# Statistics, casts and attention loads of a two-block layer spread over turns: one core, float32 in two parts

## The chip, the cores and the metric

One NeuronCore of a Trainium2 chip runs the whole program. The metric is the device time of one execution in microseconds (us), median of three runs. Engines are named as the profile names them: PE is TensorE (PEld its weight loads), DVE is VectorE, ACT is ScalarE, POOL is GpSimd, SP is SyncE, which here only starts transfers.

## What is computed

Two blocks, each on 1024 tokens of width 1024, in float32. The first block, shortened:

```python
h = rms_norm(x, norm_g)
u = h @ w_in                       # v_c b_c c_c z_c q k v z_a gate_logits
y_a = (b_c * causal_conv(c_c * v_c) * silu(z_c)) @ w_conv_out
q, k = rms_norm(q, q_norm_g), rms_norm(k, k_norm_g)    # 16 and 4 heads of 64
o = sliding_window_attention(q, k, v, sinks) * silu(z_a)   # window 128, blocks of 128
y_b = o @ w_attn_out
merged = sigmoid(g_a) * y_a + sigmoid(g_b) * y_b
x = x + merged @ w_out
```

The second block adds to x a mixer (pooling and gated linear attention), a cross attention to 256 memory tokens, and a feed-forward layer of width 2816 with a causal convolution, each behind its own norm; the last step is a norm.

## The kernel before

Features lie on the 128 partitions, tokens along the rows, in two halves of 512. An activation is a grid of 8 feature tiles by 2 halves. Every matrix product is taken in three matmuls: each operand is split into a high part (a cast on ACT) and a low part (a subtraction on DVE), and high x high, high x low and low x high are summed in PSUM (`mm3`).

Large projections of the first block and the feed-forward layer go through `wino`: two output tiles of both halves by seven products of four feature tiles each (12 matmuls a product, 84 in all) instead of eight. The products want four sums or differences of activation tiles, T1 to T4, in high and low parts. `sums` makes them: T1 = T3's first tile less T1's, and so on, four tiles each. A product whose T is not ready spins through turns (`while b not in X: tick()`).

The order of the work is written out by hand. `tick()` is a **turn**: it finishes a weight page's low part, advances the making of a pair's weights by a step, and advances each generator in the list `side` by one `yield`. Dense products call it in their middle and after their end, `wino` after each product. Each engine works in the order of the program; a wait stops all that stands behind it on that engine.

The order in the first block is: k and v from x itself (the norm's factor is applied later), while `second_half` and `x_thread` make hT, the normalised x, half by half; z of the attention (four tiles dense, then pairs with `wino`); four pairs of q; four pairs of the gates; sixteen of the convolution; four more of the gates; then `co`, the convolution's output product, 8 weight pages per half, during which the generator `attention` runs in turns; then `ao`, the attention's output product.

`hT_sums` waits until hT is complete, loads all 16 tiles of hT again from DRAM copies (`hraw`, stored by `x_thread`) and runs `sums` on them in place. In the feed-forward layer `ffn_norm` runs `sums` on its own tiles.

`q_out` evacuates one q tile: ACT squares it (`qsq`), ACT writes the high part, DVE the low part. Its generator `stats` stores both parts to DRAM, gives the squares to PE (L882, head sums by a block of ones), and DVE and POOL make the norm's factor from that. It is advanced in the turn that follows the evacuation at once.

`att_in(p, h)` loads what one half of the heads p needs for one half of the tokens h: keys, four q tiles in two parts, values (for p = 0), four z tiles: 14 or 16 transfers, issued on POOL's queue. For h = 0 both calls stand ahead of the attention, for h = 1 inside it, at units 9 and 17. A `Unit` is a block of 128 queries and four heads; in turn i unit i makes scores, unit i - 1 the exponentials and the normalisation (POOL, L1103), unit i - 2 the transposes, unit i - 3 the values. In the first block of queries `scores` fills the score tile with a memset on POOL (L1066), and DVE then copies the valid scores into it (L1078).

Tiles come from rotating pools: `hp` 64 tiles of 512 columns, `tp` 8, `wpool` 2 per kind of weight page, and a region that is closed and opened again between stages (`hq`, `pg`). A tile is used again when its last reader is done. Weight pages (512 KB) are loaded on SP, two ahead.

Of the kernel before, what the change touches and what calls it, by code (L numbers as in the profile page):

```python
# [11 lines left out]
ALU = mybir.AluOpType  # L12
# [5 lines left out]
HT = 512  # L18
# [98 lines left out]
def _body(es, tc, nc, wp, vec, xT, memT, gk2, pw, cst, out, dbg):  # L117
# [9 lines left out]
    V, S, G, T = nc.vector, nc.scalar, nc.gpsimd, nc.tensor  # L127
# [29 lines left out]
    def dram(s, shape=(P, HT)):  # L157
        n = nm(s)
        return dpool.tile(list(shape), F32, name=n, tag=n)
# [8 lines left out]
    def f(ap):  # L168
        return ap.bitcast(F32)
# [6 lines left out]
    side = []  # L176
# [269 lines left out]
    def sums(t, X, hts):  # L446


        at = {"T1": (0, 0), "T2": (4, 1), "T3": (0, 1), "T4": (4, 0)}
        his, los = {}, {}  # L450

        def u(name, k):
            return t[at[name][0] + k, at[name][1]]

        def hi(name, k):
            his[name, k] = hts[name](name, F32R)
            S.copy(his[name, k], u(name, k))

        def lo(name, k):
            los[name, k] = hts[name](name, F32R)  # L460
            V.tensor_tensor(los[name, k], u(name, k), f(his[name, k]), ALU.subtract)  # L461
            if k == 3:
                X[name] = [(his[name, i], los[name, i]) for i in range(4)]

        for k in range(4):
            V.tensor_tensor(u("T1", k), u("T3", k), u("T1", k), ALU.subtract)
            V.tensor_tensor(u("T3", k), u("T3", k), u("T2", k), ALU.subtract)
            hi("T1", k)
            yield
        for k in range(4):  # L470
            V.tensor_tensor(u("T2", k), u("T2", k), u("T1", k), ALU.subtract)
            lo("T1", k)
            hi("T2", k)
            yield
        for k in range(4):
            lo("T2", k)
            V.tensor_tensor(u("T4", k), u("T4", k), u("T2", k), ALU.subtract)
            hi("T3", k)
            yield
        for k in range(4):  # L480
            lo("T3", k)
            hi("T4", k)
            if k:
                lo("T4", k - 1)
            yield
        lo("T4", 3)

    def reload(items, s, first=4, per=2, lag=3):

# [150 lines left out]
    xs = grid(KT)  # L640
# [27 lines left out]


    hR, hT = grid(KT), grid(KT)  # L670
    hraw = {}
    nrms = [Norm(), Norm()]
    rx = [None, None]

# [12 lines left out]
    def x_thread(h):  # L687

        rx[h] = rstd_cols([nrms[h].acc], 4, D, "o")
        for _ in range(3):  # L690
            yield
        R = bcast_cols(rx[h], 4, "s")
        yield
        sp = Splits(pool=True)
        for kt in range(KT):
            t = tp("xn")
            V.scalar_tensor_tensor(t, xs[kt][h], col("norm_g", kt), R, ALU.mult, ALU.mult)
            hT[kt][h] = [None, None]
            sp.add(t, hT[kt][h], "xn")
            hraw[kt, h] = dram("hraw")  # L700
            nc.sync.dma_start(hraw[kt, h], t)
            if kt % 2:
                yield
        sp.flush()

    kp = [(pg("kh", F32R), pg("kl", F32R)) for _ in range(2)]
# [125 lines left out]

    XB = {}

    def hT_sums():
        while None in [x[1] for x in hT] or len(kd) < 8 or len(vd) < 4:
            yield
        reopen("q1pool", 16)
        t = {}
        order = [(kt, h) for k in range(4) for kt, h in ((k, 0), (k, 1), (k + 4, 1))] + [(k, 0) for k in range(4, 8)]  # L840

        def loads():
            for i, (kt, h) in enumerate(order):
                t[kt, h] = (hp if (kt < 4) == (h == 0) or kt == 7 else hq)("ht")
                nc.sync.dma_start(t[kt, h], hraw[kt, h])
                if i in (3, 7, 9, 11, 13):
                    yield

        g = loads()
        for _ in range(3):  # L850
            next(g)
            yield
        side.append(g)
        yield from sums(t, XB, {"T1": hp, "T2": hp, "T3": hq, "T4": hq})


    zd, qd, rqt = {}, {}, {}
    gbd, gad, ycd = grid(KT), grid(KT), grid(KT)
# [7 lines left out]
    def q_out(p, j, h, o):  # L866
        if (p, h) not in rqt:
            rqt[p, h] = spool.tile([P, 4, 4, 2], F32, name=nm("rq"), tag="rq", bufs=4)
        rq = rqt[p, h]
        sq = tp("qsq")  # L870
        S.activation(sq, o, AF.Square)
        qh, ql = tp("qh", F32R), tp("ql", F32R)
        S.activation(qh, o, AF.Copy, scale=col("q_norm_g"))
        V.scalar_tensor_tensor(ql, o, col("q_norm_g"), f(qh), ALU.mult, ALU.subtract)
        qd[p, j, h] = dram("qdh"), dram("qdl")

        def stats():
            for dst, src in zip(qd[p, j, h], (qh, ql)):
                nc.sync.dma_start(dst, f(src))
            st = ps("t", (P, 4, 64))  # L880
            for t in range(4):
                T.matmul(st[:, t, :], sq[:, t * P:(t + 1) * P], blk2.rearrange("p a b -> p (a b)"), start=True, stop=True)  # L882
            ms = sm("ms", (P, 8))

            V.tensor_scalar(ms.rearrange("p (a b) -> p a b", b=2), st[:, :, 0:64:32], 1.0, 64 * EPS, ALU.mult, ALU.add)
            G.tensor_tensor(rq[:, :, j, :], ms.rearrange("p (a b) -> p a b", b=2),
                            mhalf.rearrange("p (a b) -> p a b", b=2), ALU.pow)
            return
            yield

        side.append(stats())

# [128 lines left out]

    def att_in(p, h):

        if h == 0:
            kp[p] = pg("kh", F32R), pg("kl", F32R)
        for i in range(2):
            nc.gpsimd.dma_start(f(kp[p][i][:, h * HT:(h + 1) * HT]), kd[p, h, i])
        for j in range(4):
            qT[p, j, h] = hp("qh", F32R), hp("ql", F32R)
            for i in range(2):  # L1030
                nc.gpsimd.dma_start(f(qT[p, j, h][i]), qd[p, j, h][i])
            if j == 1 and p == 0:
                vv[h] = pg("vh", F32R, (P, 4, 256)), pg("vl", F32R, (P, 4, 256))
                for i in range(2):
                    nc.gpsimd.dma_start(f(vv[h][i]), vd[h, i])
        for j in range(4):
            oT[p][j][h] = hp("o")
            nc.gpsimd.dma_start(oT[p][j][h], zd[p, j, h])

    class Unit:  # L1040

# [16 lines left out]
        def scores(self):  # L1058
            p, n, h = self.p, self.n, self.h
            kh, kl = kp[p]  # L1060
            qc = self.qc
            pr = tp("pr", shape=(P, 4, P))
            c0 = 0 if n else P
            kc = slice((n - 1) * P + c0, (n + 1) * P)
            if n == 0:
                G.memset(pr, -1e30)  # L1066
            s = [ps("s", (P, 2, 256)) for _ in range(2)]
            for jj in range(2):
                qh, ql = qT[p, self.js.start + jj, h]
# [84 lines left out]
    def attention():  # L1154
# [1 line left out]
        n = len(units)  # L1156
        todo = []
        dv = None
        for _ in range(3):
            yield  # L1160
        for i in range(n + 3):
            if 0 <= i - 1 < n:
# [11 lines left out]
                units[i - 2].turn()  # L1174
            if i < n:
                units[i].scores()
            if i in (9, 17):
                att_in(i // 16, 1)
            if todo:
                p, j, h = todo.pop(0)  # L1180
                osp[4 * p + j][h] = split(oT[p][j][h], "o")
# [13 lines left out]
            d[m, h] = hp("g")  # L1195
            eng.dma_start(d[m, h], src[m][h])

    for p in range(2):
        att_in(p, 0)
    gate_in(gin, gad, 0, 0)  # L1200
    while None in [yc[c][0] for c in range(KT)]:
        tick()
    side.append(attention())
# [836 lines left out]
```

## Time and profile before

| | |
|---|---|
| median of 3 runs | 2487.8 us (2484.42 to 2496.45) |
| profiled execution | 2496.5 us, its span 2494.7 us |
| PE busy | 2394.4 us, 96% |
| DVE, ACT, POOL busy | 1471.7, 1010.2, 608.5 us |
| DMA | 269.17 MB, mean 108 GB/s |

A busy PE is at its peak only where the granted clock is 1.00; the clock has two levels, 1.2 and 2.4 GHz, and a stretch's figure is the mean of them (0.5 and 1). Times of the views are in us from the start of the span. "Idle before" is the time that the engine stood still ahead of an instruction, with what ended it.

### The profile page before, as it was taken

The page shows a single profiled execution, that of the slowest core. Times are in us where ns is not written, and L with a number is a line of the kernel's source. Part 1 is how long each engine was busy: PE and PEld are TensorE (multiplying, and loading weights), DVE is VectorE, ACT ScalarE, POOL GpSimd, SP SyncE. Part 2 cuts the span into 40 slices and gives each one's busy share as a digit, 9 for nine tenths or more (in the row PEclk, how much of TensorE's full clock was granted, in tenths as well). Part 3 has the DMA queues.
Part 4 walks back from the last instruction along what each step waited for, and adds up shares of the span by engine and source line. Part 5 has one row for each costly group of instructions (what it writes and reads, how often), then busy time and mean ns, then how long its engine had stood idle before and what let it go on. Part 6 is the DMA issues. An engine that isn't in the chain of part 4 may idle for free. (4 is left out here: it accounts for less than half of the span.)

```text
span 2494.7 us, 30966 instructions
## 1 busy us (share of the span) xinstructions
PE 2394.4 (96%) x11550; PEld 1959.4 (79%) x11550; DVE 1471.7 (59%) x2303; ACT 1010.2 (40%) x1871; POOL 608.5 (24%) x629
## 2 busy tenths in 40 slices
PE   8988899999997889999999999999999999999998
PEld 7866688888885677887887888888878888878887
DVE  6642336666634778646435556455677878874335
ACT  5433343333343666334512334344455555562212
POOL 3234432333313555022001020001204233310003
PEclk9999999999998999999999999999999999999999
DMA  4622231211246533641100235322522222244322
GB/s 164 249 93 102 102 110 60 80 65 68 68 136 231 190 133 104 211 145 61 51 28 28 76 115 165 120 70 89 169 65 80 81 96 77 76 140 151 101 78 89
DMA packets 106231, 269.17 MB, mean 108 GB/s; under 512 B 12352, under 2 KB 14816, under 8 KB 106080
## 3 DMA queue, kind: packets, MB, share of 16 engines
q1 hardware_dynamic: 98544, 244.11, 29.1%
q0 software_dynamic: 6992, 22.55, 2.5%
q8 instruction: 91, 1.49, 0.2%
q10 hardware_dynamic: 544, 0.52, 0.1%
q14 instruction: 60, 0.49, 0.1%
HBM read 205.28 MB, written 61.87 MB: 107 GB/s over the span
## 5 line engine op out<-in xcount | busy, mean ns | idle before, releaser
L411 PE MATMUL pss<-T,wsh 128*128 128x512 f32 x588 | 232.4, 395 | 9.2 <-DVE T L461 9.2
L410 PE MATMUL pss<-T,wsh 128*128 128x512 f32 x588 | 236.6, 402 | 2.0 <-DVE cb L991 1.2
L345 DVE TENSOR_TENSOR wl<-wr,wh 128x1024 fp32r<-128x1024 f32 (+1 forms) x147 | 177.3, 1206 | 99.2 <-ACT wh L281 99.1
L412 PE MATMUL pss<-T,wsl 128*128 128x512 f32 x588 | 232.6, 396 | 0.0
L566 POOL TENSOR_TENSOR sq<-sq,sq 128x512 f32<-128x512 f32 (+1 forms) x58 | 70.9, 1223 | 610.2 <-ACT sq L562 609.1
L298 POOL TENSOR_TENSOR ws<-wr 128x512 f32<-128x512 f32 x49 | 70.8, 1445 | 586.4 <-DMA wr<-in_wp_dram 468.3
L330 DVE TENSOR_TENSOR wsl<-ws,wsh 128x512 fp32r<-128x512 f32 x196 | 188.1, 1000 | 33.4 <-ACT wsh L312 32.4
L281 ACT CAST wh<-wr 128x1024 fp32r<-128x1024 f32 (+1 forms) x147 | 148.2, 1008 | 143.0 <-PE psmm L382 133.1
L381 PE MATMUL psmm<-xnh,wh 128*128 128x512 f32 x448 | 179.5, 401 | 3.0 <-ACT wh L281 3.0
L383 PE MATMUL psmm<-xnh,wl 128*128 128x512 f32 x448 | 176.0, 393 | 1.3 <-DVE wl L345 1.3
L382 PE MATMUL psmm<-xnl,wh 128*128 128x512 f32 x448 | 176.0, 393 | 1.1 <-POOL u L1735 0.8
L412 PE MATMUL psmm<-xnh,wl 128*128 128x512 f32 x392 | 154.0, 393 | 1.6 <-DVE wl L302 1.6
L410 PE MATMUL psmm<-xnh,wh 128*128 128x512 f32 x392 | 154.6, 394 | 0.0
L411 PE MATMUL psmm<-xnl,wh 128*128 128x512 f32 x392 | 153.4, 391 | 0.0
L411 PEld LDWEIGHTS pss<-T,wsh 128*128 128x128 f32 x588 | 112.2, 191 | 34.1 <-DVE T L461 10.5
L410 PEld LDWEIGHTS pss<-T,wsh 128*128 128x128 f32 x588 | 111.9, 190 | 32.0 <-ACT pss L417 5.1
L412 PEld LDWEIGHTS pss<-T,wsl 128*128 128x128 f32 x588 | 112.0, 191 | 25.8
L383 PE MATMUL psmm<-fh,wl 128*128 128x512 f32 (+1 forms) x300 | 116.0, 387 | 1.1 <-DVE wl L345 1.1
L381 PE MATMUL psmm<-fh,wh 128*128 128x512 f32 (+1 forms) x300 | 116.0, 387 | 0.0
L382 PE MATMUL psmm<-fl,wh 128*128 128x512 f32 (+1 forms) x300 | 115.9, 386 | 0.0
L562 ACT ACTIVATE sq<-x 128x512 f32<-128x512 f32 (+1 forms) x80 | 47.1, 588 | 165.3 <-DVE x L1255 110.5
L302 DVE TENSOR_TENSOR wl<-wr,wh 128x1024 fp32r<-128x1024 f32 x49 | 60.9, 1243 | 85.9 <-ACT wh L296 85.9
(453 smaller groups left out, 6288.9 us busy)
## 6 DMA issues: line engine op xcount, KB each, us to landing
wr<-in_wp_dram SPq DMA_DIRECT2D x238, 512.0 KB, 3.7
act<-fa SPq DMA_DIRECT2D x44, 256.0 KB, 2.0
fr<-act SPq DMA_DIRECT2D x44, 256.0 KB, 4.6
wr<-in_wp_dram SPq DMA_DIRECT2D x24, 384.0 KB, 3.2
xd<-x SPq DMA_DIRECT2D x32, 256.0 KB, 4.4
x<-xd SPq DMA_DIRECT2D x32, 256.0 KB, 4.0
x<-in_xT_dram SPq DMA_DIRECT2D x16, 256.0 KB, 5.7
hraw<-xn SPq DMA_DIRECT2D x16, 256.0 KB, 2.3
```

Of the source, the lines that this page charges most:

```text
L281: S.copy(hi[:, :n], raw[:, :n])
L298: G.tensor_tensor(sg[0], a21, a22, ALU.add)
L302: V.tensor_tensor(l12, r1, f(h12), ALU.subtract)
L330: V.tensor_tensor(lo, raw, f(hi), ALU.subtract)
L345: V.tensor_tensor(lo, raw, f(hi), ALU.subtract)
L381: T.matmul(out_ap, lh, rh, start=first, stop=False)
L382: T.matmul(out_ap, lh, rl, start=False, stop=False)
L383: T.matmul(out_ap, ll, rh, start=False, stop=last)
L410: T.matmul(o, lh, rh, start=first and kt == 0, stop=False, skip_group_check=True)
L411: T.matmul(o, lh, rl, start=False, stop=False, skip_group_check=True)
L412: T.matmul(o, ll, rh, start=False, stop=kt == 3, skip_group_check=True)
L566: eng.tensor_tensor(self.acc, self.acc, sq, ALU.add)
```

## The change

1. `sums` works in 18 turns. Turn i makes the difference number i, casts the one of the turn before, and takes the low part of the one before that. The sixteen casts and low parts go through T1, T2, T3, T4 in order.
2. In `x_thread` the second half of hT is written over its x tile and stays there; it is no longer stored and loaded. `hT_sums` loads the first half alone: tiles 0 to 3 in two turns before hT is complete, tiles 4 to 7 one per turn beside `sums`.
3. `stats` yields once before its first step, so stores and head sums of a q tile come one turn later.
4. `att_in` is a generator on SP's queue with a pair of transfers per turn. Its first three steps stand ahead of the attention, the others go into `side`; for h = 1 it starts at units 8 and 16. The attention's first unit comes one turn later (4 instead of 3).
5. The memset of `scores` goes to DVE.

```diff
-        for k in range(4):
-            V.tensor_tensor(u("T1", k), u("T3", k), u("T1", k), ALU.subtract)
-            V.tensor_tensor(u("T3", k), u("T3", k), u("T2", k), ALU.subtract)
-            hi("T1", k)
-            yield
...
+        for i in range(18):
+            if 2 <= i and i - 2 < 16:
+                j = i - 2
+                lo(order[j // 4], j % 4)
+            if 1 <= i < 17:
+                j = i - 1
+                hi(order[j // 4], j % 4)
+            k = i % 4
+            if i < 4:
+                V.tensor_tensor(u("T1", k), u("T3", k), u("T1", k), ALU.subtract)
+                V.tensor_tensor(u("T3", k), u("T3", k), u("T2", k), ALU.subtract)
...
+            yield
...
-            t = tp("xn")
+            t = xs[kt][h] if h else tp("xn")
...
-            hraw[kt, h] = dram("hraw")
-            nc.sync.dma_start(hraw[kt, h], t)
+            if h:
+                ht[kt, h] = t
+            else:
+                hraw[kt] = dram("hraw")
+                nc.sync.dma_start(hraw[kt], t)
...
     def hT_sums():
+        for k in range(4):
+            ht_in(k, hp)
+            if k % 2:
+                yield
...
+        side.append(ht_rest())
+        yield from sums(ht, XB, {"T1": hp, "T2": hp, "T3": hq, "T4": hq})
...
         def stats():
+            yield
             for dst, src in zip(qd[p, j, h], (qh, ql)):
                 nc.sync.dma_start(dst, f(src))
...
+        def two(a, b):
+            for dst, src in zip(a, b):
+                nc.sync.dma_start(dst, src)
...
-                nc.gpsimd.dma_start(f(qT[p, j, h][i]), qd[p, j, h][i])
+            two([f(t) for t in qT[p, j, h]], qd[p, j, h])
+            yield
...
-                G.memset(pr, -1e30)
+                V.memset(pr, -1e30)
...
-        for _ in range(3):
+        for _ in range(4):
             yield
...
-            if i in (9, 17):
-                att_in(i // 16, 1)
+            if i in (8, 16):
+                side.append(att_in(i // 16, 1))
...
-    for p in range(2):
-        att_in(p, 0)
     gate_in(gin, gad, 0, 0)
+    first = att_in(0, 0)
+    for _ in range(3):
+        next(first)
+
+    def rest():
+        yield from first
+        yield from att_in(1, 0)
+
+    side.append(rest())
```

How it moves instructions, at the three places that matter. On PE, in a pair of q: `psmm` is the first product's bank, complete with its third row here, and `pss` the next product. Before, the squares of the tile in `psmm` stand behind it at once:

```order
L410 MATMUL psmm_1612<-xnh_656,wh_1479 128x512
L411 MATMUL psmm_1612<-xnl_657,wh_1479 128x512
L412 MATMUL psmm_1612<-xnh_656,wl_1500 128x512
L882 MATMUL pst_1711<-blk_81,qsq_1693 128x64 x4
L410 MATMUL pss_1625<-T_305_1265,wsh_1552 128x512
```

And now (the head sums are L879 here), the last rows of the next product of 12 matmuls stand ahead of the squares:

```order
L410 MATMUL pss_1585<-T_297_1271,wsh_1512 128x512
L411 MATMUL pss_1585<-T_303_1294,wsh_1512 128x512
L412 MATMUL pss_1585<-T_297_1271,wsl_1534 128x512
L879 MATMUL pst_1698<-blk_81,qsq_1653 128x64 x4
L410 MATMUL pso_1628<-xnh_844,wsh_1513 128x512
```

The 12 rows of the product into `pss` stood behind the squares of `psmm` and stand ahead of them now.

On DVE, at the end of the sums of the first block: `T` is a low part made from a raw sum (`ht`, now also `x`) and its cast, `wl` and `wsl` are low parts of weights, `c` is an evacuation of the first pair. Before:

```order
L330 TENSOR_TENSOR wsl_1396<-ws_1326,wsh_1385 128x512
L461 TENSOR_TENSOR T_347_1398<-ht_1023,T_321_1321 128x512
L461 TENSOR_TENSOR T_349_1402<-ht_1113,T_343_1390 128x512
L461 TENSOR_TENSOR T_350_1404<-ht_1087,T_327_1334 128x512
L461 TENSOR_TENSOR T_352_1408<-ht_1132,T_348_1400 128x512
L902 TENSOR_TENSOR c_353_1422<-pss_1286,q_316_1310 128x512
L461 TENSOR_TENSOR T_356_1428<-ht_1134,T_351_1406 128x512
```

And now:

```order
L462 TENSOR_TENSOR T_303_1294<-x_127,T_297_1271 128x512
L302 TENSOR_TENSOR wl_1312<-wr_1206,wh_1288 128x1024
L462 TENSOR_TENSOR T_310_1320<-ht_999,T_304_1296 128x512
L314 TENSOR_TENSOR wsl_1344<-wr_1208,wsh_1318 128x512
L462 TENSOR_TENSOR T_319_1350<-ht_1020,T_311_1322 128x512
L897 TENSOR_TENSOR c_321_1366<-pss_1263,q_299_1286 128x512
```

Before, the last low parts of T3 and T4 stand together, ahead of the evacuation of the product that uses T3; now T3's last low part stands three rows of other work and one or two turns ahead of it, and T4's are spread among low parts of weights.

On POOL, at the attention's start: `ql` and `o` are loads of `att_in`, `pr` the score tile. Before, the memset and the normalisation stand behind all loads of both calls (28; the last ones shown):

```order
L1031 DMA ql_6007<-qdl_2421 128x512
L1038 DMA o_6010<-zd_1378 128x512
L1038 DMA o_6012<-zd_1462 128x512
L1038 DMA o_6014<-zd_1546 128x512
L1038 DMA o_6016<-zd_1610 128x512
L1066 MEMSET pr_6092 128x512
L1103 TENSOR_TENSOR pr_6092<-pr_6092,den_6139 128x512
```

And now the loads stand on SP, in pairs between a weight page (`wr`), a gate (`g`) and the store of a merged tile (`mcd`):

```order
L1021 DMA qh_5928<-qdh_1756 128x512
L1021 DMA ql_5929<-qdl_1757 128x512
L241 DMA wr_5935<-in_wp_dram 128x1024
L1197 DMA g_5937<-gad_5450 128x512
L1021 DMA vh_5953<-vd_903 128x1024
L1021 DMA vl_5954<-vd_905 128x1024
L1224 DMA mcd_5970<-g_5918 128x512
L1021 DMA qh_5972<-qdh_1864 128x512
```

Nothing of POOL's queue stands ahead of the score tile's work any more, and SP's weight pages have pairs of loads around them. POOL has 64 instructions fewer (60 loads and 4 memsets), SP 44 more (60 loads, less 8 stores and 8 loads of hT), DVE 4 more.

## Rows read from the trace of the kernel before

**Rows 1.** Page, engines: busy us, share of the span, instructions.
```profile
PE 2394.4 (96%) x11550; PEld 1959.4 (79%) x11550; DVE 1471.7 (59%) x2303; ACT 1010.2 (40%) x1871; POOL 608.5 (24%) x629
```

**Rows 2.** Waits of PE, whole span: total us, times, longest us.
```profile
PE pst L882 <- ACT qsq L871: 17.9, 16, 1.5
PE pss L1073 <- DVE pr L1078: 13.3, 1, 13.3
PE pso L1146 <- ACT pch L1125: 9.3, 4, 6.5
PE pss L411 <- DVE T L461: 9.2, 3, 3.6
PE pst L1123 <- POOL pr L1103: 7.0, 1, 7.0
...
PE psmm L381 <- ACT wh L281: 3.0, 1, 3.0
```

**Rows 3.** Stretches: length, PE, PEld, DVE, ACT, POOL busy, clock, DMA share, GB/s.
```profile
130.00:180.00 50.00, 42.98 (x169) 34.37 (x170) 25.23 (x27) 17.68 (x30) 14.44 (x10) 0.90 0.25 88
180.00:305.00 125.00, 107.10 (x476) 84.99 (x475) 36.82 (x65) 42.11 (x71) 52.14 (x32) 0.92 0.27 101
305.00:760.00 455.00, 453.80 (x1979) 370.57 (x1978) 250.67 (x297) 165.81 (x272) 138.31 (x100) 1.00 0.25 86
760.00:820.00 60.00, 46.04 (x244) 34.84 (x244) 29.40 (x79) 23.58 (x77) 26.19 (x47) 0.89 0.68 248
820.00:880.00 60.00, 51.84 (x288) 39.51 (x288) 48.74 (x132) 37.19 (x118) 32.42 (x53) 0.91 0.49 172
880.00:960.00 80.00, 73.53 (x432) 58.35 (x429) 64.10 (x184) 49.94 (x171) 46.99 (x77) 0.96 0.38 132
...
1790.00:1870.00 80.00, 73.12 (x314) 57.83 (x314) 62.02 (x89) 43.49 (x68) 12.89 (x15) 0.98 0.24 80
```

**Rows 4.** Timeline of PE after the 13.3 us wait: start us, duration us.
```profile
790.50 0.63 PE L382 MATMUL psmm<-ycl,wh 128*128 128x512 f32 x1
790.93 0.48 PE L383 MATMUL psmm<-ych,wl 128*128 128x512 f32 x1
```

**Rows 5.** Timeline of PE, head sums of q, with idle time before.
```profile
183.98 1.10 PE L882 MATMUL pst<-blk,qsq 128*128 128x64 f32 x8 [0.74 <-ACT qsq L871]
189.40 1.11 PE L882 MATMUL pst<-blk,qsq 128*128 128x64 f32 x8 [1.50 <-ACT qsq L871]
...
276.83 1.10 PE L882 MATMUL pst<-blk,qsq 128*128 128x64 f32 x8 [0.75 <-ACT qsq L871]
```

**Rows 6.** DMA issues from 180 to 305 us: count, KB, median us to landing.
```profile
qdh<-qh SPq DMA_DIRECT2D x16, 256.0 KB, 2.0
```

**Rows 7.** Timeline of ACT, feed-forward layer's sums.
```profile
1828.29 0.62 ACT L457 CAST T<-ft 128x512 fp32r<-128x512 f32 x1 [2.94 <-DVE ft L471]
```

**Rows 8.** Timeline of POOL during the attention.
```profile
757.75 0.63 POOL L1027 DMA_DIRECT2D kh<-kd  x1 [39.33 <-PE pss L412]
...
785.76 0.54 POOL L1066 MEMSET pr<- 128x512 f32 x1
...
841.09 0.58 POOL L1027 DMA_DIRECT2D kh<-kd  x1
...
853.53 2.04 POOL L1103 TENSOR_TENSOR pr<-pr,den 128x512 f32<-128x512 f32 x2
```

**Rows 9.** Weight pages and gates: DMA issues, 757 to 960 us, then SP and ACT.
```profile
wr<-in_wp_dram SPq DMA_DIRECT2D x16, 512.0 KB, 3.7
...
g<-gad SPq DMA_DIRECT2D x16, 256.0 KB, 3.9
...
801.29 0.33 SPq L241 DMA_DIRECT2D wr<-in_wp_dram  x1
...
809.01 1.05 ACT L281 CAST wh<-wr 128x1024 fp32r<-128x1024 f32 x1
```

**Rows 10.** DMA queues from 757 to 960 us: packets, MB, share.
```profile
q0 software_dynamic: 5056, 16.78, 22.3%
```

More of the change, by code (lines that the diff above doesn't have):

```diff
@@ L449, in sums @@
         at = {"T1": (0, 0), "T2": (4, 1), "T3": (0, 1), "T4": (4, 0)}
+        order = ("T1", "T2", "T3", "T4")
         his, los = {}, {}
@@ L463, in lo @@
                 X[name] = [(his[name, i], los[name, i]) for i in range(4)]
-        for k in range(4):
-            V.tensor_tensor(u("T1", k), u("T3", k), u("T1", k), ALU.subtract)
-            V.tensor_tensor(u("T3", k), u("T3", k), u("T2", k), ALU.subtract)
-            hi("T1", k)
-            yield
[L470 to L473, printed above, removed]
-            yield
[L475 to L486, printed above, removed]
+        for i in range(18):
[9 more added lines that the diff above has]
+                V.tensor_tensor(u("T3", k), u("T3", k), u("T2", k), ALU.subtract)
+            elif i < 8:
+                V.tensor_tensor(u("T2", k), u("T2", k), u("T1", k), ALU.subtract)
+            elif i < 12:
+                V.tensor_tensor(u("T4", k), u("T4", k), u("T2", k), ALU.subtract)
+            yield
     def reload(items, s, first=4, per=2, lag=3):
@@ L670, in _body @@
     hR, hT = grid(KT), grid(KT)
-    hraw = {}
+    hraw, ht = {}, {}
     nrms = [Norm(), Norm()]
@@ L833, in _body, with ht_in @@
     XB = {}
+    def ht_in(kt, pool):
+        ht[kt, 0] = pool("ht")
+        nc.sync.dma_start(ht[kt, 0], hraw[kt])
     def hT_sums():
+        for k in range(4):
+            ht_in(k, hp)
+            if k % 2:
+                yield
         while None in [x[1] for x in hT] or len(kd) < 8 or len(vd) < 4:
@@ L838, in hT_sums, with ht_rest @@
         reopen("q1pool", 16)
[L839 to L849, printed above, removed]
-        for _ in range(3):
-            next(g)
+        side.append(ht_rest())
+        yield from sums(ht, XB, {"T1": hp, "T2": hp, "T3": hq, "T4": hq})
+    def ht_rest():
+        for k in range(4, 8):
+            ht_in(k, hp if k == 7 else hq)
             yield
-        side.append(g)
-        yield from sums(t, XB, {"T1": hp, "T2": hp, "T3": hq, "T4": hq})
     zd, qd, rqt = {}, {}, {}
@@ L887, in stats @@
                             mhalf.rearrange("p (a b) -> p a b", b=2), ALU.pow)
-            return
-            yield
         side.append(stats())
@@ L1022, in att_in @@
     def att_in(p, h):
+        def two(a, b):
+            for dst, src in zip(a, b):
+                nc.sync.dma_start(dst, src)
         if h == 0:
             kp[p] = pg("kh", F32R), pg("kl", F32R)
-        for i in range(2):
-            nc.gpsimd.dma_start(f(kp[p][i][:, h * HT:(h + 1) * HT]), kd[p, h, i])
+        two([f(t[:, h * HT:(h + 1) * HT]) for t in kp[p]], [kd[p, h, i] for i in range(2)])
+        yield
         for j in range(4):
             qT[p, j, h] = hp("qh", F32R), hp("ql", F32R)
-            for i in range(2):
-                nc.gpsimd.dma_start(f(qT[p, j, h][i]), qd[p, j, h][i])
+            two([f(t) for t in qT[p, j, h]], qd[p, j, h])
+            yield
             if j == 1 and p == 0:
                 vv[h] = pg("vh", F32R, (P, 4, 256)), pg("vl", F32R, (P, 4, 256))
[L1034 to L1038, printed above, removed]
+                two([f(t) for t in vv[h]], [vd[h, i] for i in range(2)])
+                yield
+        for j in range(0, 4, 2):
+            for i in (j, j + 1):
+                oT[p][i][h] = hp("o")
+            two([oT[p][i][h] for i in (j, j + 1)], [zd[p, i, h] for i in (j, j + 1)])
+            yield
     class Unit:
@@ L1158, in attention @@
         dv = None
-        for _ in range(3):
+        for _ in range(4):
             yield
```

## The prediction

> **What bounds the kernel now.** I read four views in this order. The page's busy times come first: TensorE works 96% of the span and no other engine comes near it [rows 1]. So only what TensorE loses can be won, and it loses in two ways: it sits idle, or it works at the lower clock. The second view, who TensorE waited for over the whole span, says where it sat idle [rows 2]. The reader is to see that the list is short: the query statistics (L882) 17.9 us in 16 waits, one wait of 13.3 us in front of the attention's scores (L1073), four waits of 9.3 us in all for values (L1146), of which one is 6.5 us, 9.2 us in three waits for the sums T of the seven-product scheme (L411), one wait of 7.0 us for a transpose (L1123), one of 3.0 us for a weight page's cast (L281). The third view, busy times by stretch with the granted clock, says what the lower clock costs [rows 3]. From 305 to 760 us the same kind of products run with almost no wait: 453.8 us busy for 1979 matmuls, 0.229 us each, clock 1.00. After a wait the matmuls start 0.43 us apart [rows 4], so a stretch at the lower of the two levels (1.2 instead of 2.4 GHz) does half the work, and the time lost to the clock is (1 - granted clock) x length. That gives 125 x 0.08 = 10.0 us for 180 to 305 us, 50 x 0.10 = 5.0 for 130 to 180, 60 x 0.11 = 6.6 for 760 to 820, 60 x 0.09 = 5.4 for 820 to 880, 80 x 0.04 = 3.2 for 880 to 960, 80 x 0.02 = 1.6 for 1790 to 1870. The fourth view is the order of time on the engines that TensorE waited for, below.
>
> **The statistics a turn later.** Each q result is squared on ScalarE and the squares go to TensorE at once, so TensorE stands still for the evacuation: 0.74 us where ScalarE reads PSUM itself, 1.50 us where a VectorE subtraction or addition comes first [rows 5]. There are 16 of them. The change puts one product of 12 matmuls in between, 12 x 0.229 = 2.7 us, more than the 1.50 us it has to cover. So 17.9 us of waits go, and with them 10.0 us of clock: 27.9 us. A second way: the period of one pair is (276.83 - 183.98) / 3 = 31.0 us [rows 5], its work 84 x 0.229 + 4 x 1.10 = 23.6 us, so 7.4 us too long, four times 29.6 us. I take 27.5, leaving 0.4 for what may remain. The stores of qh and ql move with the statistics, on SP's queue. They hold two of the eight rotating tiles for one product longer; the tile is wanted again at the earliest 24 matmuls (5.5 us) after its store is issued (that is the order of the changed program), and a store lands after 2.0 us [rows 6]. Cover 3.5 us, so no cost; without it each of the 16 would give its wait back.
>
> **The sums.** Now one turn makes a difference on VectorE, casts it on ScalarE and takes the low part on VectorE, engine waiting for engine, and the last parts of T2, T3 and T4 are late for their products: 9.2 us [rows 2] and 5.0 us of clock, 14.2. The change puts a turn between the steps, starts three turns earlier (the three turns of loads are gone) and keeps the second half of hT in its x tiles, so 8 stores and 8 loads of 256 KB fall away. T1 is ready in its 6th turn where the 11th was needed, T2 in the 10th for the 15th, T3 in the 14th for the 19th, T4 in the 18th for the 20th. Only T4's last low part comes close: it stands on VectorE behind a subtraction and two weight low parts, during the product that uses it. Bounds 0 and 1.5 us (like the waits of [rows 5]), taken 0.7. Sum: 13.5. The removed transfers are on nobody's path that TensorE waited for; nothing for them, bounds -2 and +2 us. The tiles that x now keeps longer come out of 64; the program's order shows no load or cast that waits for a matmul close before it, so nothing.
>
> The same function serves the FFN. There ScalarE stood 2.94 us for a difference made in the same turn, with the cast of a weight page queued behind it [rows 7]; that is the 3.0 us wait [rows 2], with 1.6 us of clock. VectorE is busy 62.0 of 80 us there [rows 3], so part may come back as another wait: bounds 0 and 5, taken 3.5.
>
> **The attention's loads.** POOL issues 28 loads from 757.75 us and reaches the score tile's memset only at 785.76 [rows 8]; VectorE's masked copy waits for that memset, and TensorE's next scores for the copy: 13.3 us. Each issue occupies POOL 0.54 us, and between them POOL waits for earlier loads to land. The second call (16 loads from 841.09) holds the normalisation back to 853.53 [rows 8]: 7.0 us. The third burst, 14 loads, repeats it: 6.5 us. So 26.8 us of idle and 6.6 + 5.4 + 3.2 = 15.2 us of clock, 42.0 in all. The change takes all 60 loads off POOL, spreads them over turns on SP, three or four turns ahead of use, and the four memsets go to VectorE, which has 29.4 of 60 us busy there [rows 3]; at 0.54 us each (POOL's row, VectorE's is not in the trace) they cost it about 2 us, hidden. What is late next: SP. It is paced by VectorE's low parts and by the products' results anyway; behind each pair of loads stand a weight page, a gate load and a store of the merged half. A weight page has 809.01 - 801.29 = 7.7 us from its issue to its cast and lands in 3.7 [rows 9], a reserve of 4.0 us; a 256 KB load lands 3.9 us after its issue [rows 9], and two of them now stand ahead of it, but transfers overlap. The first keys wait on SP for the last seven-product pair, as they did on POOL. One more turn before the first unit costs nothing while dense products fill it. For small new waits I take 3 us (the three other waits of L1146 are 2.8), bounds 0 and 20. Sum: 39.
>
> The Trainium skill, page "DMA: Bandwidth & Descriptors", section "Issuing engines are not separate DMA queues", speaks against this part: the same 16 DMA engines carry the loads whoever starts them, and another issuer saves only its time for issuing, which it calls usually small. By that the attention's gain would not come, which is all of rival (a) below; the rows say that here the issuing is the wait, since the memset behind it reads no loaded data.
>
> **Sum.** 27.5 + 13.5 + 3.5 + 39 = 83.5 us. The profiled execution took 2496.5 us (span 2494.7 and 1.8 around it): 2413.0. It stands 8.7 us above the median of the runs, 2487.8 (2484.4 to 2496.5); taken off the median it is 2404.3. I forecast 2405 us.
>
> **Rivals.** (a) The attention's gaps are half or wholly the loads themselves: SP, with 8 transfers in flight at most by its rotating semaphores, brings them as late as POOL did. Half the 39 us back gives 2425, all of it 2444. For it: these loads are 16.8 MB in this stretch [rows 10], and they stay. Against it: TensorE's waits end at POOL's own work. (b) The eight rotating tiles stop ScalarE in the q stage, since stores are a turn later: 2405 + 27.5 = 2432. Against it: the 3.5 us of cover. (c) The sums gain nothing, because VectorE's low parts of weights come between: 2405 + 13.5 + 3.5 = 2422. (d) Slower: weight pages come late behind attention loads on the one queue. Four loads per page at 3.9 us each, one after another, are 15.6 us, less the reserve 4.0 is 11.6 us for each of the 16 pages of the convolution's output product: 186 us, 2591. It decides from 4.0 us per page on, and the kernel is slower than before from 4.0 + 83 / 16 = 9.2 us. Against it: the transfers overlap, and SP has nearly 8 us per page. The Trainium skill, same page, section "Queues, rings and completion order", has a rule for it: each DMA engine takes turns between queues, packet by packet. So before, a weight page on SP's queue shared with POOL's loads, and now it stands behind them; no run here shows that yet.
>
> **How the numbers follow.** Forecast as summed, 2392 to 2420: 0.75. (a) 0.12 (all of it 0.03), (b) 0.05, (c) 0.04, (d) 0.04. The low end: every bound at its best (29.6 + 16.2 + 5 + 42 = 92.8) off the fastest run is 2391.6, and a few waits of [rows 2] that I left alone may shrink with them: 2387. The high end takes in (b), (c) and half of (a): 2438; outside it lie all of (a) and (d), and a little below. A measurement tells about 0.5% (12 us) from no change. (d) is the only slower case, 0.04, and 0.02 stays for cases that cancel: faster 0.94, same 0.02, slower 0.04.
>
> **What would show it.** Right: no wait of TensorE for the squares, clock 1.00 from about 165 us to the attention's end, no POOL DMA between 700 and 950 us, no wait over 2 us at the scores and transposes. Wrong: ScalarE's squares waiting for landings (b); waits for a weight page's cast at the dense products beside the attention (d); scores waiting for keys or queries (a); TensorE still waiting for T (c).

## The result

The changed kernel takes 2418.3 us (median; 2415.36 to 2421.36) where the kernel before takes 2488.1 beside it: a ratio of 0.9715, 95% interval 0.9686 to 0.9744; the medians lie 69.8 us apart. The forecast was 2405 with a range of 2387 to 2438. Sign and size are right; the gain came out 13.7 us smaller than the 83.5 us of the sum, and two of its terms were sized wrongly in ways that can be read from the rows.

The profiled execution of the changed kernel has a span of 2419.6 us (2421.4 for the run) against 2494.7 (2496.5). First the engines, from its page (busy us, share of the span, instructions; they answer to [rows 1]):

```profile
PE 2374.0 (98%) x11550; PEld 1949.9 (81%) x11550; DVE 1481.5 (61%) x2307; ACT 1009.5 (42%) x1871; POOL 574.8 (24%) x565
```

TensorE's idle time fell from 100.3 to 45.6 us, its busy time by 20.4 us. Next its waits over the whole span (total us, times, longest us; they answer to [rows 2]):

```profile
PE psmm L381 <- ACT xrh L673: 6.0, 1, 6.0
PE psmm L381 <- DVE kg L735: 4.3, 1, 4.3
PE pss L411 <- DVE T L462: 3.5, 1, 3.5
PE psmm L383 <- DVE wl L345: 3.2, 4, 1.2
PE pso L1147 <- POOL pph L1134: 2.4, 5, 0.6
...
PE pss L1074 <- DMA qh<-qdh: 1.5, 1, 1.5
...
PE pso L1147 <- ACT oh L376: 1.1, 1, 1.1
```

The five long entries of [rows 2] are gone: no wait for the squares, none of 13, 7 or 6.5 us in the attention, none for the feed-forward's weight cast. The first two entries that are left lie at the start of the program and were there before. New or left over are one wait of 3.5 us for T and one of 1.5 us for queries.

The stretches that answer to [rows 3] (length, PE, PEld, DVE, ACT, POOL busy, clock, DMA share, GB/s): the first block's seven-product pairs, q, the rest up to the convolution's output product, three of the attention, one of the feed-forward layer:

```profile
120.30:164.80 44.50, 40.98 (x173) 33.20 (x172) 25.40 (x25) 19.64 (x34) 18.56 (x12) 0.96 0.27 92
164.80:290.00 125.20, 125.20 (x613) 105.17 (x612) 49.83 (x78) 56.51 (x93) 57.94 (x38) 1.00 0.37 133
...
720.00:780.00 60.00, 58.34 (x328) 46.67 (x327) 43.00 (x112) 34.53 (x106) 19.43 (x28) 0.97 0.82 296
780.00:840.00 60.00, 57.05 (x319) 43.38 (x317) 55.39 (x150) 39.58 (x131) 28.44 (x41) 0.97 0.52 173
840.00:889.00 49.00, 49.00 (x297) 39.40 (x297) 44.85 (x126) 34.13 (x117) 29.41 (x44) 1.00 0.47 162
```

q runs without a gap at full clock. POOL issues no transfer in the attention any more. All of them stand on SP's queue now, and the transfer engines are busy to 0.82 in the first 60 us of it (0.68 in [rows 3]) without a long wait of TensorE.

**Where the time went.** All kernels here do the same work in the same order, so I cut each trace at the same five instructions of TensorE: the products that fill the banks, the first of q, the first matmul of `co`, the first scores of the cross attention, and the last bank-filling product, in the feed-forward layer. The lengths in us, each worked out from the start times of these instructions (e1 to e3 are the experiments below, each with one part of the change alone):

| stage | before | after | less by | forecast | e1 statistics | e2 sums | e3 attention |
|---|---|---|---|---|---|---|---|
| to the first block's pairs | 119.2 | 120.3 | -1.1 | 0 | 119.6 | 118.3 | 118.1 |
| first block's pairs, with T | 52.9 | 44.5 | 8.5 | 13.5 | 46.9 | 41.8 | 54.0 |
| q, gates, convolution | 586.6 | 555.2 | 31.3 | 27.5 | 553.9 | 585.1 | 586.5 |
| `co` with the attention, then on | 844.3 | 815.0 | 29.3 | 39 | 846.2 | 846.7 | 814.3 |
| cross attention to the feed-forward | 262.5 | 256.8 | 5.7 | 3.5 | 262.6 | 256.7 | 262.3 |
| the rest | 629.2 | 627.8 | 1.4 | 0 | 629.8 | 628.6 | 629.3 |

The stages that an edit doesn't touch agree within 2.5 us from trace to trace, except the first block's pairs: without the edit to the sums they take 46.9 to 54.0 us in five profiles, with it 41.8 to 44.5 in five. So that stage's 8.5 us is known to a few us only (the means of the two groups, 51.1 and 42.7 us, lie 8.4 apart), and the others to about 2.

### The profile page after: what moved, and what is told of

Same layout as the page of the kernel before. It is cut to its first block, busy times and chain, and to the rows that moved or that the text cites. A ratio compares the mean times of both kernels' runs of the same rounds, so it can differ in the third digit from the quotient of the medians.

```text
span 2419.6 us, 30915 instructions
## 1 busy us (share of the span) xinstructions
PE 2374.0 (98%) x11550; PEld 1949.9 (81%) x11550; DVE 1481.5 (61%) x2307; ACT 1009.5 (42%) x1871; POOL 574.8 (24%) x565
## 5 line engine op out<-in xcount | busy, mean ns | idle before, releaser
L410 PE MATMUL pss<-T,wsh 128*128 128x512 f32 x588 | 233.6, 397 | 2.0 <-DVE cb L986 1.2
L411 PE MATMUL pss<-T,wsh 128*128 128x512 f32 x588 | 229.7, 391 | 3.5 <-DVE T L462 3.5
L561 POOL TENSOR_TENSOR sq<-sq,sq 128x512 f32<-128x512 f32 (+1 forms) x58 | 70.9, 1223 | 610.4 <-ACT sq L557 609.5
```

The costliest lines, as they stand in the source:

```text
L410: T.matmul(o, lh, rh, start=first and kt == 0, stop=False, skip_group_check=True)
L411: T.matmul(o, lh, rl, start=False, stop=False, skip_group_check=True)
L561: eng.tensor_tensor(self.acc, self.acc, sq, ALU.add)
```

## The experiments

**Three parts, one at a time.** Each of the first three kernels is the kernel before with one part of the diff. How many us a kernel takes less is one minus its ratio, times the median of the kernel before that stood beside it.

e1, the statistics a turn later:

```diff
         def stats():
+            yield
             for dst, src in zip(qd[p, j, h], (qh, ql)):
...
         side.append(stats())
-            return
-            yield
```

> The kernel before with one edit: the query statistics a turn later. Theory A (the prediction's term: 17.9 us of waits and 10.0 us of clock): 27.5 us less, about 2460.5. Theory B (the two traces cut at the stage's ends, 31.2 us from the first q pair to the end of the ga pages): about 2457. If the parts help each other (the full change needed for it), less than 25 us. In the trace: no wait of TensorE for the squares at 180 to 305 us, clock 1.00 there; the other waits as before.

Measured: 2462.6 us, ratio 0.9886 (0.9869 to 0.9903), 28.4 us less. The stage itself is 32.7 us shorter. The whole stage before and in e1 (columns as above):

```profile
172.15:758.70 586.55, 567.45 (x2482) 460.96 (x2481) 288.68 (x362) 210.03 (x346) 189.15 (x130) 0.98 0.26 89
```

```profile
166.50:720.40 553.90, 553.79 (x2481) 455.17 (x2480) 290.73 (x362) 210.14 (x346) 188.38 (x130) 1.00 0.27 94
```

19.0 us of it are idle time (17.9 for the squares, and one wait of 1.2 for another tile that also fell away) and 13.7 us are busy time. The forecast had 10.0 us for the latter, all clock. The rest is in how a wait is counted. The matmul ahead of the first wait of [rows 5], in the kernel before:

```profile
182.85 0.39 PE L412 MATMUL psmm<-xnh,wl 128*128 128x512 f32 x1
```

It lasts 0.39 us, while matmuls that follow one another start 0.229 us apart. The idle time of 0.74 us counts from its end; from start to start TensorE lost 1.13 - 0.23 = 0.90. So each wait costs 0.16 us more than the list of waits says, 2.6 us for 16 of them, and 10.0 + 2.6 = 12.6 of the 13.7. Both theories stand within the interval; the part doesn't need the others.

e2, the staged sums, the second half of hT kept in its x tiles, eight loads for sixteen (the diff of the change without the statistics and the attention):

> The kernel before with the staged sums, the second half kept in its x tiles and the eight loads of hT that are left. Theory A (13.5 in the first block, 3.5 in the FFN): 17 us less, about 2471. Theory B (the traces cut at the stages' ends: 8.6 in the first block, 1.5 to 5 in the FFN): 10 to 13 us less, about 2476. Theory B also expects a wait of about 3.5 us for T4's last low part near 143 us; theory A one of 0 to 1.5 us.

Measured: 2477.6 us, ratio 0.9949 (0.9932 to 0.9966), 12.7 us less. Theory B: 10 to 13. The trace has one wait of 2.4 us for T4's last low part. What makes it late is in e7.

e11, of e2 only the staging (`sums` as after; all sixteen tiles stored and loaded again):

> The kernel before with the staged sums alone: all sixteen tiles of hT are still stored and loaded again, and the sums start three turns later than in the changed kernel. Theory A (the staging carries the gain): as with both, 12 to 13 us less, about 2477. Theory B (the three turns that the loads took are needed too: T4's last low part then comes a turn behind its product): nothing in the first block or a loss there, only the FFN's 6 us, about 2484, and a wait for T of 4 us or more at 140 to 150 us.

Measured: 2484.4 us, ratio 0.9970 (0.9957 to 0.9983), 7.5 us less, the first block's pairs 46.1 us where e2 has 41.8. There, TensorE's waits for T:

```profile
134.38 0.50 PE L411 MATMUL pss<-T,wsh 128*128 128x512 f32 x1 [1.52 <-DVE T L462]
136.18 0.50 PE L411 MATMUL pss<-T,wsh 128*128 128x512 f32 x1 [0.83 <-DVE T L462]
141.67 0.51 PE L411 MATMUL pss<-T,wsh 128*128 128x512 f32 x1 [0.18 <-DVE T L462]
143.36 0.50 PE L411 MATMUL pss<-T,wsh 128*128 128x512 f32 x1 [0.72 <-DVE T L462]
145.06 0.50 PE L411 MATMUL pss<-T,wsh 128*128 128x512 f32 x1 [0.73 <-DVE T L462]
```

The time is nearer to theory B's, some 6 us less from the feed-forward layer alone, than to theory A's 12 to 13. The waits sum to the 4.0 us that theory B names, though they are spread: the first two before T3's last two tiles, the last three before the first three of T4. So the staging without the three earlier turns keeps the products waiting for one low part after another, and keeping x in place is worth some 4 to 5 us there. That this comes from the three turns and not from the transfers themselves is what the waits suggest; no kernel has the one without the other.

e3, the loads over SyncE in turns and the memsets on VectorE:

> The kernel before with the attention's loads over SyncE in turns and the memsets on VectorE, and nothing else. Theory A (26.8 us of idle and the clock formula, 15.2, less 3): 39 us less, about 2449. Theory B (idle time goes as forecast, but the lower clock cost these small products less than (1 - clock) x length): 27 to 31 us less, about 2459. If POOL's issuing were not the wait (the loads' own landing), no more than 20 us less, 2468 or more.

Measured: 2459.4 us, ratio 0.9875 (0.9857 to 0.9894), 31.1 us less, as theory B says. The stage of `co` before and in e3:

```profile
758.70:1603.00 844.30, 806.02 (x4298) 654.48 (x4297) 500.24 (x969) 345.39 (x741) 196.39 (x287) 0.98 0.36 120
```

```profile
758.60:1572.90 814.30, 800.24 (x4298) 649.44 (x4297) 505.81 (x973) 344.81 (x741) 169.43 (x224) 1.00 0.37 124
```

Of the 30.0 us, 38.28 - 14.06 = 24.2 are idle time and 5.8 are busy time. The forecast had 26.8 - 3 = 23.8 of idle time, which is right, and 15.2 us for the clock, which is not. The three parts alone sum to 28.4 + 12.7 + 31.1 = 72.2 us, and the whole change's ratio gives 70.9: they add up, so within the intervals (about 4 us for each part) nothing is given back between them.

**What the low clock costs.** The kernel before, cut finely around the wait of 13.3 us, shows where the low clock lies:

```profile
777.00:780.00 3.00, 0.00 (x0) 0.00 (x0) 0.00 (x0) 0.00 (x0) 1.37 (x3) 0.58 1.05 411
780.00:784.00 4.00, 0.00 (x0) 0.00 (x0) 0.00 (x0) 0.00 (x0) 3.11 (x7) 0.50 1.02 382
784.00:786.80 2.80, 0.00 (x0) 0.00 (x0) 0.47 (x2) 0.00 (x0) 1.93 (x4) 0.50 1.02 382
786.80:791.20 4.40, 4.37 (x18) 3.72 (x19) 2.96 (x8) 2.12 (x9) 0.05 (x1) 0.51 0.51 163
791.20:795.00 3.80, 3.80 (x26) 2.89 (x26) 2.18 (x7) 0.19 (x2) 1.45 (x2) 1.00 0.46 176
```

Clock 0.50 holds from about 777.5 to 791.2 us, 13.7 us in all, but only 4.4 us of these have matmuls in them [rows 4]; the other 9.3 are idle time that the list of waits has counted already. (1 - clock) x length charges both: 6.9 us where 2.2 were lost. Two kernels measure this by itself: the changed kernel with one artificial wait in front of the third ga pair, where nothing else waits.

```diff
+        if m == 4:
+            d = ps("t")
+            hi = XB["T1"][0][0]
+            T.matmul(d, hi[:, :P], hi, start=True, stop=True)
+            a = sm("stl", (P, 16), 2)
+            V.tensor_copy(a, d[:, :16])
+            for _ in range(K):     # K = 1 in e9, 5 in e10
+                b = sm("stl", (P, 16), 2)
+                G.dma_start(b, a)
+                a = b
+            T.transpose(ps("t")[:16, :P], a, ident)
         pair(("ga", m), ("ga", m + 1), XB, ...)
```

> The changed kernel with one wait put in front of the third pair of the ga pages, where nothing else waits: a product, a copy of 16 of its columns, one small transfer on POOL's queue, a transpose that reads what landed. A wait of 2 to 3 us. Theory A (the clock costs (1 - granted clock) x length of the low stretch): the idle time and half of the low stretch, which is about 3.4 us: 1.7 more. Theory B (only the part of the low stretch in which matmuls run costs): also 1.5 to 2, since the low stretch lies behind the wait.

> The same with five such transfers one after another: a wait of 10 to 13 us. Theory A: half of a low stretch of about 13 us, so 6 to 7 us beyond the idle time. Theory B: the low stretch lies for the most part inside the wait and costs only behind it: 4 us or so of matmuls 0.43 us apart, 2 to 2.5 us beyond the idle time.

Measured: one run each, 2419.2 and 2431.7 us; the traces say more. e9, the wait and the matmuls behind it:

```profile
679.54 0.28 PE L1020 MATMUL pst<-ident,stl 128*16 128x128 f32 x1 [2.81 <-DMA stl<-stl]
679.57 0.47 PE L410 MATMUL psmm<-xnh,wh 128*128 128x512 f32 x1
679.88 0.39 PE L411 MATMUL psmm<-xnl,wh 128*128 128x512 f32 x1
680.11 0.40 PE L412 MATMUL psmm<-xnh,wl 128*128 128x512 f32 x1
```

After 2.8 us of idle time the matmuls go on 0.23 us apart, and the stretches of the wait and behind it have the full clock, which neither theory expected:

```profile
676.50:679.50 3.00, 0.23 (x2) 0.00 (x0) 0.17 (x1) 0.69 (x1) 2.16 (x3) 1.00 0.35 128
679.50:683.00 3.50, 3.46 (x16) 2.88 (x17) 0.00 (x0) 0.33 (x1) 3.50 (x3) 1.00 0.01 2
```

e10, the stretches around the wait, and its end:

```profile
675.00:678.00 3.00, 0.29 (x2) 0.00 (x0) 0.17 (x1) 0.69 (x1) 0.63 (x1) 0.90 0.36 135
678.00:682.00 4.00, 0.00 (x0) 0.00 (x0) 0.00 (x0) 0.00 (x0) 1.07 (x2) 0.50 0.02 4
682.00:686.60 4.60, 0.00 (x1) 0.00 (x1) 0.00 (x0) 0.00 (x0) 2.16 (x3) 0.50 0.02 5
686.60:691.00 4.40, 4.40 (x11) 3.50 (x12) 0.00 (x0) 0.00 (x0) 3.92 (x4) 0.50 0.00 0
```

```profile
686.60 0.38 PE L1020 MATMUL pst<-ident,stl 128*16 128x128 f32 x1 [11.31 <-DMA stl<-stl]
...
690.62 0.60 PE L410 MATMUL psmm<-xnh,wh 128*128 128x512 f32 x1
691.05 0.40 PE L411 MATMUL psmm<-xnl,wh 128*128 128x512 f32 x1
691.29 0.39 PE L412 MATMUL psmm<-xnh,wl 128*128 128x512 f32 x1
```

A wait of 11.3 us, a low stretch of 13.6 us, of which 4.4 hold work. The ten matmuls from 686.63 to 691.05 took 4.42 us where ten take 2.29: 2.1 us lost, theory B, not the 6.8 us of the formula. The Trainium skill, page "TensorE: Matmul & The Clock Gate", section "HAM oscillation — how this bites in real kernels", has the same formula, the throttled time times one half; taken over all 13.6 us at half clock it gives 6.8 us beyond the wait. The measurement decides: it holds for the part of the low stretch that has matmuls in it. In the query statistics that is the whole of it, which is why the formula was right there. The first such stretch of the kernel before, busy all through:

```profile
190.00:193.50 3.50, 3.50 (x13) 2.83 (x13) 2.02 (x4) 0.00 (x0) 1.40 (x1) 0.55 0.39 150
```

**Which part of the attention's edit it is.** The edit has two halves, and e4, e5 and e3 are three corners of a square whose fourth is the kernel before.

e4, the four memsets on VectorE, the loads still in bursts on POOL:

```diff
             if n == 0:
-                G.memset(pr, -1e30)
+                V.memset(pr, -1e30)
```

> The kernel before with the four memsets on VectorE alone; the loads stay on POOL in their bursts. Theory A (the memset's place behind the loads is the 13.3 us wait): the wait at the first scores goes, with its clock 15 to 19 us less, about 2471. Theory B (POOL's normalisation of the first unit stands behind the same loads, until about 786 us): the wait comes back in front of the transposes, 2488 within 5 us. The waits of 7.0 and 6.5 us behind the second and third bursts stay in both.

Measured: 2483.6 us, ratio 0.9973 (0.9958 to 0.9989), 6.7 us less, between the two theories. TensorE's waits (whole span), and what POOL and TensorE do near 780 us:

```profile
PE pst L1123 <- POOL pr L1103: 13.9, 2, 7.3
PE pso L1146 <- ACT pch L1125: 8.6, 3, 6.1
```

```profile
780.06 2.04 POOL L1103 TENSOR_TENSOR pr<-pr,den 128x512 f32<-128x512 f32 x2
```

```profile
781.16 1.11 PE L1123 MATMUL pst<-ident,pr 128*128 128x128 f32 x4 [6.61 <-POOL pr L1103]
```

The 13.3 us at the scores are gone, and the same burst now holds POOL's normalisation, so half comes back two turns later at the transposes; the waits behind the second and third burst stay. In the burst the transfer engines are full (share 1.02 to 1.05 from 777 to 787 us in the kernel before, above), POOL stands still between its issues until earlier loads have landed, and its own work stands behind them for 28 us.

e5, the loads in turns on SyncE, the memsets still on POOL:

> The kernel before with the attention's loads over SyncE in turns; the four memsets stay on POOL (the fourth corner beside the loads and the memsets together and the memsets alone). Theory A (everything on POOL was late only because it stood behind the loads): the same as with both, 31 us less, about 2459, and no wait at the first scores but for loads. Theory B (the memset's move has a part of its own, the 6.7 us that it gave alone): about 2466.

Measured: 2462.1 us, ratio 0.9884 (0.9853 to 0.9914), 28.9 us less, with no wait for the memset. Within the intervals that is e3's 31.1; theory B's 2466 lies inside it too, and the profile's stage, 819.7 us against 814.3, leaves room for a few us in the memsets, so that is not settled. What it does show is that most of the gain comes without the memsets' move. The attention's start one turn later and the second half's loads one unit earlier are part of e3 and e5 and were not run apart.

e6, the changed kernel with these loads issued by POOL again, in the same turns (`two` in `att_in` with `nc.gpsimd` for `nc.sync`):

> The changed kernel with the attention's loads in the same turns but issued by POOL again. Theory A (the burst is the cost: two loads a turn hold POOL about 1.1 us, less than a turn): within 5 us of the changed kernel, 2416 to 2423. Theory B (POOL's issues also stand still until an earlier load has landed, and the normalisation behind them each time): the waits at the transposes and values come back in many small pieces, 2430 or more.

Measured: 2420.0 us, ratio 0.9709 (0.9681 to 0.9738): the changed kernel's own time within the intervals. Its stage of `co` is 818.7 us long where the changed kernel has 815.0, with waits for POOL of 4.0 us in ten pieces for 2.4 in five, so the queue that issues them makes a few us at most; the burst was the cost, by standing ahead of POOL's own work. The Trainium skill's rule in the prediction, that another issuer saves only its time for issuing, agrees with this trace as far as it goes; what it leaves out is the work that stands behind the issues.

**Why T4 is late.** In the changed kernel, VectorE and then POOL around 140 us, and TensorE's wait:

```profile
138.19 3.46 DVE L330 TENSOR_TENSOR wsl<-ws,wsh 128x512 fp32r<-128x512 f32 x2
141.57 1.74 DVE L462 TENSOR_TENSOR T<-ht,T 128x512 fp32r<-128x512 f32 x1
```

```profile
138.13 1.29 POOL L298 TENSOR_TENSOR ws<-wr 128x512 f32<-128x512 f32 x1 [10.12 <-DMA wr<-in_wp_dram]
139.50 1.59 POOL L299 TENSOR_TENSOR ws<-ws,wr 128x512 f32<-128x512 f32 x1
141.06 1.70 POOL L305 TENSOR_TENSOR ws<-wr,wr 128x512 f32<-128x512 f32 x1
```

```profile
143.37 0.50 PE L411 MATMUL pss<-T,wsh 128*128 128x512 f32 x1 [3.52 <-DVE T L462]
```

T4's last low part is the second row: 1.74 us where the same instruction elsewhere takes 0.68, behind two weight low parts of 3.46 where they take 1.28, while POOL sums the next pair's weights. In e2, e6, e9 and e10, whose order is the same here, the pair takes 2.38 and the wait is 2.4 us, so 3.5 is the worst of five. The trace of the kernel before had such lengths already, four low parts of T beside POOL's sums, where two beside an idle POOL take 1.28:

```profile
139.54 5.90 DVE L461 TENSOR_TENSOR T<-ht,T 128x512 fp32r<-128x512 f32 x4
```

e7 holds POOL back until that low part is there:

```diff
             S.copy(h12, r1)
+            self.made = getattr(self, "made", 0) + 1
+            if self.made == 3:
+                G.tensor_copy(sm("ms", (P, 8))[:, :1], f(XB["T4"][3][1][:, :1]))
```

> The changed kernel with POOL's sums of the next weight pair held back in the first block until T4's last low part is there (a one-column copy of that part stands ahead of them on POOL). Theory A (VectorE's low parts are stretched because POOL works at the same time, 3.46 for 1.28 and 1.74 for 0.68 us): they take 1.28 and 0.68 us, the wait of 3.5 us for T4 falls to under 0.7 and the half clock behind it goes: about 5 us less than the changed kernel, 2413. Theory B (it is VectorE's order alone, or what these instructions read): the wait stays at 3 us or more, 2418.

Measured: 2414.7 us, ratio 0.9690 (0.9659 to 0.9721). VectorE, then POOL:

```profile
135.14 1.28 DVE L333 TENSOR_TENSOR wsl<-ws,wsh 128x512 fp32r<-128x512 f32 x2
136.34 0.69 DVE L465 TENSOR_TENSOR T<-ht,T 128x512 fp32r<-128x512 f32 x1
```

```profile
137.09 0.19 POOL L299 COPY ms<-T 128x1 f32<-128x1 f32 x1 [11.42 <-DVE T L465]
137.23 1.29 POOL L301 TENSOR_TENSOR ws<-wr 128x512 f32<-128x512 f32 x1
138.61 1.29 POOL L302 TENSOR_TENSOR ws<-ws,wr 128x512 f32<-128x512 f32 x1
```

With POOL idle VectorE takes 1.28 and 0.69 us; with VectorE idle POOL takes 1.29 for each sum where it took 1.59 and 1.70. The wait for T4 falls to 0.28 us and the stage from 44.5 to 39.6 us: theory A. That rests on the traces; the ratios of e7 and of the changed kernel overlap. The Trainium skill, page "SBUF — State Buffer", section "SBUF: two separate sides", says that a VectorE instruction with two inputs in SBUF and a GpSimd instruction that reads SBUF take turns at one port pair, and that the loser waits for the whole instruction; the pair of engines is the one seen here, and the rows agree: in the changed kernel the two weight low parts end at 141.65 us, 0.56 after POOL's second sum (141.09), and T4's at 143.31, 0.55 after its third (142.76). Each ended only behind the sum that it stood beside, while POOL's own sums grew by just 0.30 and 0.41 us.

**Two more edits.** e8 is the changed kernel with two edits, each for a wait that it still has:

```diff
                 hi(order[j // 4], j % 4)
+                if i == 16:
+                    lo("T4", 3)
...
-            if j == 1 and p == 0:
+            if j == 3 and p == 0:
                 vv[h] = pg("vh", F32R, (P, 4, 256)), pg("vl", F32R, (P, 4, 256))
```

(and the loop that takes the low parts stops one turn earlier.)

> The changed kernel with two edits: T4's last low part right behind its cast, ahead of the weights' low parts, and the attention's v loaded behind the four q pairs instead of between them. Theory A: the wait of 3.5 us for T4 and that of 1.5 us for the queries go, with the half clock behind each: about 8 us less than the changed kernel, 2410. Theory B (VectorE then stands still for the cast, and the loads land late whatever their order): no gain, 2416 to 2420.

Measured: 2411.2 us (2409.5 to 2412.6), ratio 0.9673 (0.9647 to 0.9699). Its interval overlaps with the changed kernel's; its runs all lie below that kernel's (2415.4 to 2421.4), which stood beside other runs of the kernel before. Both waits are gone from its trace, the first block's pairs take 39.1 us for 44.5 and the stage of `co` 813.3 for 815.0: 7.1 us, a little less than the 8 us expected. The rest was not traced.

## Why the prediction was right, and where it was off

**What bounds the kernel.** Right. The profiled executions differ by 54.7 us of TensorE's idle time and 20.4 us of its busy time, and [rows 2] named the places.

**Query statistics, 27.5 us forecast.** Right in mechanism and nearly in size: 28.4 us alone. No wait is left, and no wait of ScalarE in that stage names a store, so rival (b) falls. The stage got 31 to 33 us shorter: short by the 0.16 us that each wait costs above its idle time, which the sum left out.

**Sums, first block, 13.5 us.** Right in mechanism, too large in size: 8.5 us. Two things were mis-sized. The clock term (5.0) charged idle time a second time, about 1 us: of 10.2 us at half clock there, 2.1 had no matmul in them. And the bound of 0 to 1.5 us for T4's last low part took VectorE's instructions at their usual durations; by these the part would have been late by some 0.3 us (e7), but they wait for POOL's sums, and 3.5 us of wait and 1.7 us of half clock behind it came. Rival (c), no gain at all, didn't come.

**Removed transfers, nothing.** Right in that no wait of TensorE names them. Keeping x in place, with the three turns that it frees, is worth 4 to 5 us of the first block's gain (e2 against e11); the prediction had these turns in its 13.5.

**Sums in the feed-forward, 3.5 us.** Too small: the stage is 5.7 us shorter in both kernels with the staged sums. The give-back that I allowed for, because VectorE is busy 62.0 of 80 us there [rows 3], did not come: the wait, its clock and the 0.16 are 4.8, the last 0.9 I did not trace.

**Attention, 39 us.** The cause was right and its price was not. (The first burst has 30 loads, 16 and 14, where the prediction says 28; no term used the count.) The idle time fell as forecast (24.2 for 23.8 us). The step that failed is the formula for the clock: 15.2 us were taken from (1 - granted clock) x length, and 5.8 came. [rows 4] showed half clock right behind the wait, and the matmul at 791.25 already back at 0.23 us was one row on; I read the length of the low stretch off the clock column and not off the starts. Rival (a), the loads themselves, remains as one wait of 1.5 us for queries. Rival (d), late weight pages, didn't come: no wait of TensorE for a weight cast lies in that stage, a page lands 3.8 us after its issue where it took 3.7, and ScalarE's one wait for a page, 5.0 us, made TensorE wait for no cast.

**The sum.** For the two profiled executions the sum gives 83.5 and the traces 75.1: attention 9.7 less, first block 5.0 less, start 1.1 less, statistics 3.8 more, the second block 3.6 more. The other 5.3 us between 75.1 and the 69.8 of the medians are which executions were profiled: that of before stood 8.3 us above its median, that of after 3.1. The prediction named this choice (2413.0 or 2404.3) and took the median, with waits that were read in the slower execution. The first block's pairs, 52.9 us there, take 46.9, 48.2, 53.6 and 54.0 in the four other profiles with the old sums, so the sum came out this close to the medians partly by luck: it overpriced the attention and the first block by 14.7 us and underpriced the statistics and the second block by 7.4.

## What to carry to other kernels

Price a wait of TensorE by starts: from the last matmul before it to the first one back at full rate, less what these matmuls take at full rate; the mean clock of a stretch that contains idle time counts that time twice. A burst of transfers costs by the instructions that stand behind it on its engine: spread over turns it cost a few us at most on either queue, while moving only the memsets away gave 6.7 of the 31.1 us. (A burst moved whole to SP's queue was not run.) VectorE's subtractions and POOL's sums held each other up here, so a low part that is just in time needs the duration it has beside its neighbour's work.

## What the hardware did that was not expected

- A wait of 2.8 us, alone, was followed by matmuls at full rate (e9); one of 3.5 us was followed by half clock (the changed kernel: the stretch around it has a clock of 0.96), and so were waits of 1.5 us that came close behind others in the kernel before (190.00 to 193.50 above). The same wait for T4 of 2.4 us was followed by half clock in e6 (0.50 from 143.9 to 147.3 us) and by the full clock in e2, e9 and e10. The length of one wait does not tell the clock behind it.
- A wait of 11.3 us had no longer slow work behind it than 4.4 us, the same as one of 13.3 us.
- VectorE's subtraction of two 128x512 tiles takes 0.68 us alone and 1.74 beside POOL's sums, ending some 0.55 us after the sum beside it; POOL's sum takes 1.29 alone and up to 1.7.
